# Loading float32 instead of casting in the DMA, in blocks of 8 heads with paired transposes: a change to a batched q·kᵀ kernel

## The chip, the cores and the metric

The kernel runs on one core of a Trainium2 chip. The metric is the device time in microseconds (us) of one execution. Times are medians of 4 executions for a changed kernel, and of 4 to 7 for the kernel before, which was run again on the same chip beside each group of experiments. In what follows PE is the engine that multiplies matrices, DVE (vector), ACT (scalar) and GpSimd (POOL in the profiles) are the engines that copy and convert here, and SP only issues transfers. SBUF is the memory on the chip, PSUM the one that PE writes to, and DMA stands for the transfers and the engines that carry them. A ratio is the mean time of one kernel's runs over that of the other's of the same rounds, so it is not quite the ratio of the medians that are quoted.

## The reference

```python
batch, n_heads, seq, head_dim = 8, 12, 1024, 64     # q and k: float32, 0.1 * normal
def reference(q, k):
    return np.einsum('bhid,bhjd->bhij', q, k).astype(np.float32)
```

There are 96 heads. Each takes 0.52 MB of input (q and k) and writes a 1024 x 1024 float32 matrix, 4.19 MB. In all 50.3 MB are read and 402.7 MB written.

## The kernel before

Inputs are loaded in batches of four heads (1, 1 and 2 at the start) by GpSimd, in a DMA that casts to float16 on the way. They are prefetched three batches ahead. PE transposes q and k through a 128 x 128 identity, DVE copies the transposed tiles from PSUM to SBUF, and PE multiplies. The contraction has only 64 rows, half of the array, so the kernel keeps a copy of k's transpose in both halves and lets even and odd output tiles use different halves. DVE empties three of eight output tiles, ACT five. Each head's 4 MB are stored by one DMA from SP.

```python
in_pool  = tc.tile_pool(name="in_pool", bufs=4)      # float16 inputs
out_pool = tc.tile_pool(name="out_pool", bufs=4)     # 4 heads of output, 4 MB each
...
def load(self):                                       # on GpSimd's queue, float32 -> float16
    nc.gpsimd.dma_start(out=dst[:, : self.R], in_=src[rows].rearrange("(p r) d -> p r d", p=P))
...
def transpose(self, a):                               # once per head: 4 + 16 matmuls
    for e in range(4):
        nc.tensor.transpose(t_ps[:, e], self.q_sb[:, r : r + 2], ident)
    for t in range(NT):
        nc.tensor.transpose(t_ps[0:64, 4 + t], rows, ident)
        nc.tensor.transpose(t_ps[64:128, 4 + t], rows, ident)
    ...                                               # DVE copies to qT and kT
def scores(self, g):
    for t in range(NT):
        h = (t % 2) * 64                              # halves of the array alternate
        for n in range(2):
            nc.tensor.matmul(ps[:, n * 512 : (n + 1) * 512], qT[h : h + 64, g, t // 2],
                             kT[h : h + 64, g, n * 512 : (n + 1) * 512])
        ...                                           # t in (1, 4, 6): DVE, else ACT
    nc.sync.dma_start(out=of[bh]..., in_=o_sb...)
```

## Time and profile before

| | before |
|---|---|
| time, median of 4 | 1071.33 us (1071.20 to 1072.24) |
| DMA queues, share of 16 engines | stores 88.0%, loads 11.9% |
| PE, DVE, ACT busy | 59%, 53%, 44% |
| PE on score matmuls | 480.9 us |
| four heads, while inputs are loaded | about 44 us |
| four heads, after the last load | about 39 us |

The first lines are from the page of the kernel before: busy time of the engines; the busy tenths of the DMA engines and their GB/s in 40 slices of the span; the queues (packets, MB, share); the chain of waits by engine; and three groups of instructions (busy time, mean ns of one, then idle time before them and its main releaser).

```profile
PE 627.9 (59%) x3456; PEld 214.0 (20%) x3456; DVE 565.7 (53%) x758; ACT 468.4 (44%) x481; POOL 28.2 (3%) x58
...
DMA  9999999999999999999999999999999999999996
GB/s 213 394 382 386 380 400 414 394 420 396 410 410 384 422 398 410 411 389 419 401 397 424 390 419 401 400 419 389 415 406 399 422 430 430 429 434 432 431 431 292
...
q1 hardware_dynamic: 13824, 402.66, 88.0%
q0 software_dynamic: 7488, 25.17, 11.9%
...
DMA 77%; PE 7%; ACT 7%; DVE 1%; issue 0%; ACTq 0%
...
L114 ACT COPY o_sb<-ps 128x1024 f32<-128x1024 f32 x480 | 467.1, 1014 | 566.5 <-DMA out_dram<-o_sb 359.1
L106 PE MATMUL ps<-kT,qT 64*128 64x512 f16 x1536 | 480.9, 597 | 270.8 <-ACT o_sb L114 227.2
L91 DVE COPY qT<-t_ps 128x128 f16<-128x128 f16 (+1 forms) x374 | 121.2, 469 | 95.7 <-PE t_ps L82 95.7
```

The DMA engines are the limit: nine tenths or more in every slice but the last, and 99.9% in the two queues together. ACT's idle time ends mostly when an output buffer has been stored ("DMA out_dram<-o_sb"), and PE waits for ACT. The compute engines have slack.

The next lines are from the chain of waits in order of time (start, length, what). Four heads lie between neighbours of each pair.

```profile
703.00 1.47 PE ps L106 x4
...
747.31 1.47 PE ps L106 x4
...
954.36 1.48 PE ps L106 x4
...
993.93 1.48 PE ps L106 x4
```

With loads, four heads take 44.3 us here (747.31 minus 703.00); after the last load they take 39.6 us. So eight heads with their loads cost the DMA about 88 us.

### The profile page before, as it was taken

What the parts mean: (1) busy time and instruction counts of PE and PEld (TensorE: products, weight loads), DVE (VectorE), ACT (ScalarE), POOL (GpSimd) and SP (SyncE); (2) the same over time, 40 slices, a digit from 0 to 9 for tenths busy, and PEclk for the clock granted to TensorE, in tenths of its full rate; (3) what the DMA queues carried; (4) which work ended last, traced back from release to release, by engine and by line L of the source; (5) the groups of instructions that cost most, each with busy time, mean ns of one, the idle gap of its engine ahead of it and who ended that gap; (6) DMA issues with size and microseconds to landing.
All of it is one profiled execution on the core that took longest, in us unless ns stands there. A gap on an engine that the chain in (4) does not pass through costs nothing.

```text
span 1069.6 us, 8844 instructions
## 1 busy us (share of the span) xinstructions
PE 627.9 (59%) x3456; PEld 214.0 (20%) x3456; DVE 565.7 (53%) x758; ACT 468.4 (44%) x481; POOL 28.2 (3%) x58
## 2 busy tenths in 40 slices
PE   6786455565654656557465564655656567667530
PEld 2222121121211212212122121221211212212100
DVE  5676445464653646547455464554655646655420
ACT  4454344444533445344443444444444445454530
POOL 3000000000000000000000000000000000000000
PEclk8565555555555555555555555555555555555555
DMA  9999999999999999999999999999999999999996
GB/s 213 394 382 386 380 400 414 394 420 396 410 410 384 422 398 410 411 389 419 401 397 424 390 419 401 400 419 389 415 406 399 422 430 430 429 434 432 431 431 292
DMA packets 21353, 428.39 MB, mean 401 GB/s; under 512 B 2368, under 2 KB 2880, under 8 KB 9024
## 3 DMA queue, kind: packets, MB, share of 16 engines
q1 hardware_dynamic: 13824, 402.66, 88.0%
q0 software_dynamic: 7488, 25.17, 11.9%
q8 instruction: 27, 0.44, 0.1%
q14 instruction: 14, 0.11, 0.0%
HBM read 50.33 MB, written 402.65 MB: 424 GB/s over the span
## 4 chain that ended last, share of the span: by engine, by line
DMA 77%; PE 7%; ACT 7%; DVE 1%; issue 0%; ACTq 0%
DMA out_dram<-o_sb 77%; ACT o_sb L114 7%; PE ps L106 6%; DVE kT L92 0%; DVE qT L91 0%; PE t_ps L81 0%; PE t_ps L78 0%; DVE o_sb L112 0%; PE t_ps L82 0%; ACTq L114 0%
## 5 line engine op out<-in xcount | busy, mean ns | idle before, releaser
L114 ACT COPY o_sb<-ps 128x1024 f32<-128x1024 f32 x480 | 467.1, 1014 | 566.5 <-DMA out_dram<-o_sb 359.1
L106 PE MATMUL ps<-kT,qT 64*128 64x512 f16 x1536 | 480.9, 597 | 270.8 <-ACT o_sb L114 227.2
L112 DVE COPY o_sb<-ps 128x1024 f32<-128x1024 f32 x288 | 351.7, 1223 | 374.0 <-DMA out_dram<-o_sb 213.8
L106 PEld LDWEIGHTS <-qT 64*128 64x128 f16 x1536 | 101.0, 109 | 605.2 <-issue 580.0
L91 DVE COPY qT<-t_ps 128x128 f16<-128x128 f16 (+1 forms) x374 | 121.2, 469 | 95.7 <-PE t_ps L82 95.7
L78 PE MATMUL t_ps<-ident,q_sb 128*128 128x128 f16 x384 | 56.4, 299 | 135.9 <-DVE kT L92 130.2
L92 DVE COPY kT<-t_ps 128x1024 f16<-128x1024 f16 x96 | 118.8, 1237 | 0.0
L81 PE MATMUL t_ps<-ident,k_sb 128*64 128x128 f16 x768 | 102.5, 310 | 0.0
L82 PE MATMUL t_ps<-ident,k_sb 128*64 128x128 f16 x768 | 102.4, 310 | 0.0
L81 PEld LDWEIGHTS <-k_sb 128*64 128x64 f16 x768 | 77.5, 165 | 19.8 <-issue 19.4
L82 PEld LDWEIGHTS <-k_sb 128*64 128x64 f16 x768 | 77.4, 164 | 7.5 <-issue 7.5
L78 PEld LDWEIGHTS <-q_sb 128*128 128x128 f16 x384 | 34.6, 127 | 187.2 <-issue 121.3
L64 POOL DMA_DIRECT2D q_sb<-in_q_dram x26 | 14.0, 537 | 767.5 <-PE t_ps L78 766.8
L64 POOL DMA_DIRECT2D k_sb<-in_k_dram x26 | 13.9, 534 | 13.2 <-PE t_ps L82 13.2
L114 ACT ACT_TABLE_LOAD x1 | 1.3, 1283 | 0.7 <-PEq L157 0.7
masks.py:199 POOL TENSOR_SCALAR_AFFINE_SELECT ident<-ident 128x128 f16<-128x128 f16 x1 | 0.4, 362 | 0.0
masks.py:197 POOL MEMSET ident<- 128x128 f16 x1 | 0.3, 271 | 0.0
L157 POOL MEMSET const-float32-0.0<- 128x1 f32 x1 | 0.1, 98 | 0.2 <-issue 0.2
L157 POOL MEMSET const-bfloat16-1.0<- 128x1 bf16 x1 | 0.1, 101 | 0.0
L157 POOL MEMSET const-uint8-127<- 128x1 uint8 x1 | 0.1, 101 | 0.0
L157 POOL MEMSET const-float32-1.0<- 128x1 f32 x1 | 0.1, 98 | 0.0
## 6 DMA issues: line engine op xcount, KB each, us to landing
out_dram<-o_sb SPq DMA_DIRECT2D x96, 4096.0 KB, 36.7
q_sb<-in_q_dram POOLq DMA_DIRECT2D x23, 512.0 KB, 18.1
k_sb<-in_k_dram POOLq DMA_DIRECT2D x23, 512.0 KB, 29.4
q_sb<-in_q_dram POOLq DMA_DIRECT2D x2, 128.0 KB, 3.5
k_sb<-in_k_dram POOLq DMA_DIRECT2D x2, 128.0 KB, 3.6
q_sb<-in_q_dram POOLq DMA_DIRECT2D x1, 256.0 KB, 6.3
k_sb<-in_k_dram POOLq DMA_DIRECT2D x1, 256.0 KB, 7.0
```

The costliest lines, as they stand in the source:

```text
L64: nc.gpsimd.dma_start(out=dst[:, : self.R], in_=src[rows].rearrange("(p r) d -> p r d", p=P),)
L78: nc.tensor.transpose(t_ps[:, e], self.q_sb[:, r : r + 2], ident)
L81: nc.tensor.transpose(t_ps[0:64, 4 + t], rows, ident)
L82: nc.tensor.transpose(t_ps[64:128, 4 + t], rows, ident)
L91: nc.vector.tensor_copy(out=qT[:, g, :, :, a], in_=t_ps[:, 0:4, ms])
L92: nc.vector.tensor_copy(out=kT[:, :, :, a], in_=t_ps[:, 4:12].rearrange("c t (g m) -> c g m t", g=G),)
L106: nc.tensor.matmul(ps[:, n * 512 : (n + 1) * 512], qT[h : h + 64, g, t // 2], kT[h : h + 64, g, n * 512 : (n + 1) * 512],)
L112: nc.vector.tensor_copy(out=o_sb[:, t], in_=ps)
L114: nc.scalar.copy(out=o_sb[:, t], in_=ps)
L157: nc = _bacc.Bacc("TRN2", target_bir_lowering=False, num_devices=1)
```

## The change

The intent, as far as the text of the change shows it, is to relieve PE, DVE and the casting DMA. Heads are taken in blocks of eight (2, 2 and 4 at the start), made of two halves of four. A transpose takes a row of a head from the first half beside the same row of a head from the second, 128 values wide, so two heads need 16 transposes instead of 40. Inputs are loaded as float32 by ACT's queue, one block-sized buffer (bufs=1), and GpSimd casts them to float16 just before they are transposed. Stores go out by SP and ACT in turn. The first three blocks are loaded into an output buffer that is not needed yet. A head's scores now use one half of the array for all its tiles.

```diff
-    in_pool = ctx.enter_context(tc.tile_pool(name="in_pool", bufs=4))
+    in_pool = ctx.enter_context(tc.tile_pool(name="in_pool", bufs=1))
+    half_pool = ctx.enter_context(tc.tile_pool(name="half_pool", bufs=2))
...
         def transpose(self, a):
+            t_ps = pt_pool.tile([P, 2 * NT, P], F16, tag="pt")
+            slab = slice(a * NT, (a + 1) * NT)
+            for i, src in enumerate((self.q_sb, self.k_sb)):
+                x_h = half_pool.tile([P, NT, 2, D], F16, tag=f"h{i}")
+                nc.gpsimd.tensor_copy(
+                    out=x_h, in_=src[:, :, slab].rearrange("p h t d -> p t h d")
+                )
+                for t in range(NT):
+                    nc.tensor.transpose(t_ps[:, i * NT + t], x_h[:, t], ident)
...
+            cs = slice(half * D, (half + 1) * D)
...
+                    nc.tensor.matmul(ps[:, js], qT[cs, g, t], kT[cs, g, js])
...
+            store = nc.sync if (self.first + n) % 2 == 0 else nc.scalar
...
+        for n in range(2 * b.G):
+            b.scores(n)
+            if nxt and done < nxt.G:
+                last = nxt.G if n == 2 else done + 1
+                while done < min(nxt.G, last):
+                    nxt.transpose(done)
+                    done += 1
+            if n == 3 and i + 2 < len(blocks):
+                blocks[i + 2].load(nc.scalar, nc.scalar)
```

The order of instructions on an engine is not the order of this text: the framework's scheduler decides it when the program is built.

More of the change, by code (lines that the diff above doesn't have):

```diff
@@ L28 @@
     GMAX = 4
-    assert D == 64 and NT == 8 and BH % GMAX == 0
+    assert D == 64 and NT == 8 and BH % (2 * GMAX) == 0
     qf = q.rearrange("b h s d -> (b h s) d")
@@ L37 @@
     of = out.rearrange("b h i j -> (b h) i j")
-    sizes = [1, 1, 2] + [GMAX] * (BH // GMAX - 1)
-    assert sum(sizes) == BH
+    sizes = [1, 1, 2] + [GMAX] * (BH // (2 * GMAX) - 1)
+    assert 2 * sum(sizes) == BH
     consts = ctx.enter_context(tc.tile_pool(name="consts", bufs=1))
     ident = consts.tile([P, P], F16)
-    in_pool = ctx.enter_context(tc.tile_pool(name="in_pool", bufs=4))
+    in_pool = ctx.enter_context(tc.tile_pool(name="in_pool", bufs=1))
+    half_pool = ctx.enter_context(tc.tile_pool(name="half_pool", bufs=2))
     tr_pool = ctx.enter_context(tc.tile_pool(name="tr_pool", bufs=2))
@@ L53, with place, load @@
     )
-    class Batch:
+    class Block:
         def __init__(self, first, G):
             self.first, self.G, self.R = first, G, 8 * G
-        def load(self):
-            rows = slice(self.first * S, (self.first + self.G) * S)
-            self.q_sb = in_pool.tile([P, GMAX * NT, D], F16, tag="q")
-            self.k_sb = in_pool.tile([P, GMAX * NT, D], F16, tag="k")
-            for src, dst in ((qf, self.q_sb), (kf, self.k_sb)):
-                nc.gpsimd.dma_start(
-                    out=dst[:, : self.R],
-                    in_=src[rows].rearrange("(p r) d -> p r d", p=P),
-                )
+        def place(self, q_sb, k_sb):
+            shape = dict(h=2, r=self.R, d=D)
+            self.q_sb = q_sb.rearrange("p (h r d) -> p h r d", **shape)
+            self.k_sb = k_sb.rearrange("p (h r d) -> p h r d", **shape)
+        def load(self, q_engine, k_engine):
+            if not hasattr(self, "q_sb"):
+                elems = 2 * self.R * D
+                q_sb = in_pool.tile([P, elems], F32, tag="q")
+                k_sb = in_pool.tile([P, elems], F32, tag="k")
+                self.place(q_sb, k_sb)
+            for half in range(2):
+                start = (self.first + half * self.G) * S
+                rows = slice(start, start + self.G * S)
+                for src, dst, eng in (
+                    (qf, self.q_sb, q_engine),
+                    (kf, self.k_sb, k_engine),
+                ):
+                    eng.dma_start(
+                        out=dst[:, half],
+                        in_=src[rows].rearrange("(p r) d -> p r d", p=P),
+                    )
         def alloc(self):
-            self.qT = tr_pool.tile([P, GMAX * 4 * P], F16, tag="qT")
+            self.qT = tr_pool.tile([P, GMAX * S], F16, tag="qT")
             self.kT = tr_pool.tile([P, GMAX * S], F16, tag="kT")
@@ L74, in transpose, with scores @@
             G, pp = self.G, P // self.G
-            t_ps = pt_pool.tile([P, 12, P], F16, tag="pt")
-            for e in range(4):
-                r = a * NT + 2 * e
-                nc.tensor.transpose(t_ps[:, e], self.q_sb[:, r : r + 2], ident)
-            for t in range(NT):
-                rows = self.k_sb[:, a * NT + t]
-                nc.tensor.transpose(t_ps[0:64, 4 + t], rows, ident)
-                nc.tensor.transpose(t_ps[64:128, 4 + t], rows, ident)
-            qT = self.qT[:, : G * 4 * P].rearrange(
-                "c (g e m a) -> c g e m a", g=G, e=4, m=pp
+            t_ps = pt_pool.tile([P, 2 * NT, P], F16, tag="pt")
[4 more added lines that the diff above has]
+                    out=x_h, in_=src[:, :, slab].rearrange("p h t d -> p t h d")
+                )
+                for t in range(NT):
+                    nc.tensor.transpose(t_ps[:, i * NT + t], x_h[:, t], ident)
+            qT = self.qT[:, : G * S].rearrange(
+                "c (g t m a) -> c g t m a", g=G, t=NT, a=G
             )
             kT = self.kT[:, : G * S].rearrange(
-                "c (g m a t) -> c g m a t", g=G, m=pp, t=NT
+                "c (g m a t) -> c g m a t", g=G, a=G, t=NT
             )
-            for g in range(G):
-                ms = slice(g * pp, (g + 1) * pp)
-                nc.vector.tensor_copy(out=qT[:, g, :, :, a], in_=t_ps[:, 0:4, ms])
+            nc.vector.tensor_copy(
+                out=qT[:, :, :, :, a],
+                in_=t_ps[:, :NT].rearrange("c t (g m) -> c g t m", g=G),
+            )
             nc.vector.tensor_copy(
                 out=kT[:, :, :, a],
-                in_=t_ps[:, 4:12].rearrange("c t (g m) -> c g m t", g=G),
+                in_=t_ps[:, NT:].rearrange("c t (g m) -> c g m t", g=G),
             )
-        def scores(self, g):
-            bh = self.first + g
-            qT = self.qT.rearrange("c (g e m) -> c g e m", e=4, m=P)
+        def scores(self, n):
+            half, g = divmod(n, self.G)
+            cs = slice(half * D, (half + 1) * D)
+            qT = self.qT.rearrange("c (g t m) -> c g t m", t=NT, m=P)
             kT = self.kT.rearrange("c (g j) -> c g j", j=S)
@@ L102, in scores @@
             for t in range(NT):
-                h = (t % 2) * 64
                 ps = po_pool.tile([P, S], F32, tag="po")
-                for n in range(2):
-                    nc.tensor.matmul(
-                        ps[:, n * 512 : (n + 1) * 512],
-                        qT[h : h + 64, g, t // 2],
-                        kT[h : h + 64, g, n * 512 : (n + 1) * 512],
-                    )
+                for j in range(2):
+                    js = slice(j * 512, (j + 1) * 512)
+                    nc.tensor.matmul(ps[:, js], qT[cs, g, t], kT[cs, g, js])
                 if t in (1, 4, 6):
@@ L114, in scores @@
                     nc.scalar.copy(out=o_sb[:, t], in_=ps)
-            nc.sync.dma_start(
-                out=of[bh].rearrange("(p t) j -> p (t j)", p=P),
+            store = nc.sync if (self.first + n) % 2 == 0 else nc.scalar
+            store.dma_start(
+                out=of[self.first + n].rearrange("(p t) j -> p (t j)", p=P),
                 in_=o_sb.rearrange("p t j -> p (t j)"),
             )
-    batches, first = [], 0
+    blocks, first = [], 0
     for G in sizes:
-        batches.append(Batch(first, G))
-        first += G
-    AHEAD = 3
-    for b in batches[:AHEAD]:
-        b.load()
-    make_identity(nc, ident)
-    batches[0].alloc()
-    for a in range(batches[0].G):
-        batches[0].transpose(a)
-    for i, b in enumerate(batches):
-        if i + AHEAD < len(batches):
-            batches[i + AHEAD].load()
-        nxt = batches[i + 1] if i + 1 < len(batches) else None
+        blocks.append(Block(first, G))
+        first += 2 * G
+    early_sb = out_pool.tile([P, NT, S], F32, tag="out")
+    early = early_sb.rearrange("p t j -> p (t j)")
+    at = 0
+    for b in blocks[:3]:
+        elems = 2 * b.R * D
+        b.place(early[:, at : at + elems], early[:, at + elems : at + 2 * elems])
+        at += 2 * elems
+    for b in blocks[:4]:
+        b.load(nc.sync, nc.scalar)
+    make_identity(nc, ident)
+    blocks[0].alloc()
+    blocks[0].transpose(0)
+    for i, b in enumerate(blocks):
+        nxt = blocks[i + 1] if i + 1 < len(blocks) else None
         if nxt:
             nxt.alloc()
-        for g in range(b.G):
-            b.scores(g)
-            if nxt:
-                for a in range(g * nxt.G // b.G, (g + 1) * nxt.G // b.G):
-                    nxt.transpose(a)
+        done = 0
+        for n in range(2 * b.G):
[7 more added lines that the diff above has]
+                blocks[i + 2].load(nc.scalar, nc.scalar)
 _INS = ['q', 'k']
```

## The prediction

> **What bounds the kernel now.** The DMA engines. The page's DMA slices read 9 in every tenth but the last, and the queue table gives 88.0% of the 16 engines' span to stores (402.66 MB) and 11.9% to loads. The chain of waits is 77% "DMA out_dram<-o_sb". PE is 59% busy, DVE 53%, ACT 44%; ACT's largest wait (359.1 us) is for an output buffer to be stored. From the chain, four heads take about 44.0 us while inputs are loaded and 39.3 us after the last load, so stores move at about 430 GB/s, and loading four heads (2.10 MB of float32 in HBM) costs about 4.7 us: the DMA already pays by bytes read, not by the float16 bytes written (estimate).
>
> **What the change does.**
> - *DMA.* Stores are untouched. Loads become 8 KB float32 rows without a cast; 2.10 MB at 430 GB/s is 4.9 us against 4.7 now (estimate). No gain, perhaps +0 to +4 us in all. Putting stores on two issuing queues gains nothing by itself: the Trainium skill ("DMA: Bandwidth & Descriptors", section "Issuing engines are not separate DMA queues") says that all queues run on the same 16 engines; this trace agrees, its two queues adding up to 99.9%.
> - *Transposes.* 1920 matmuls (20 per head) become 768 (16 per two heads); the DVE copies that empty them fall from 240 us to about 120 us.  Off the critical path.
> - *Scores.* Rows 0-63 and 64-127 of the array no longer alternate, so two matmuls no longer overlap. Now six 512-column matmuls take 1.92 us; alone each should take about 0.43 us at half clock (four times a 128-column transpose step of 0.105 us), so PE needs about 6.8 us per head and a head about 8 us instead of 6.7.
> - *GpSimd.* 96 casts of 128x1024, no duration in this trace; I assume 1 to 2 us each, 100 to 200 us, hidden.
> - *Bursts.* In the instruction order, three of a block's four transpose groups fall inside one head in eight. One group costs about 4.5 us (PE 2, DVE 2.5, one PSUM buffer), so that head takes some 20 us. Four output buffers hold 25 to 39 us of stores, nearly enough.
>
> **How much is on the critical path.** Almost nothing in the middle. At the start: a cast stands before the first transpose, and PE, DVE and the eleven groups of the first nine heads must keep up with 9.8 us per store; block 4's loads are issued only one to three heads before use. I expect the first store at about 22 us instead of 17.0, and 5 to 15 us of idle DMA in the first 150 us, partly paid back because float32 loads of 16 heads fill the first 20 us.
>
> **Predicted time.** 1074 us, range 1055 to 1100. Faster by over 2%: 0.03; within 2%: 0.81; slower by over 2%: 0.16.
>
> **What would show the steps right or wrong.** DMA slices still 9 throughout; about 44 us per four heads in the middle and 39.3 at the end; the DMA queue table near 88% and 11 to 12%; POOL 100 to 200 us; DMA dips, if any, before 150 us or at heads 8, 16, 24 and on.
>
> **What would make it wrong.** If GpSimd casts take 4 us or more, the bursts outlast the stores in flight and every block leaves a hole: 2 to 5% slower. If PE warms to full clock, bursts shrink and the time goes to 1065. If loads without a cast cost clearly less DMA time than 4.7 us per four heads, or the second queue lifts the rate above 430 GB/s, it could be over 2% faster; unlikely, since 453 MB at 430 GB/s are already 1053 us.

## The result, and the profile after

The changed kernel takes 1152.43 us (median of 4, 1151.28 to 1154.11): 7.6% slower (ratio 1.0756, interval 1.0738 to 1.0775). The prediction had said 1074 us, and 1055 to 1100.

The page of the changed kernel, the same lines as before, with the line of the DVE copy that moves q's transposes:

```profile
PE 757.0 (66%) x2304; PEld 286.3 (25%) x2304; DVE 510.6 (44%) x384; ACT 470.5 (41%) x481; POOL 98.1 (9%) x102
...
DMA  9969497989989989999998998998999899899998
GB/s 394 424 274 432 179 407 316 434 351 428 424 352 431 407 366 411 419 410 374 409 420 348 428 427 371 405 412 365 406 425 436 351 427 426 377 435 422 436 431 375
...
q10 hardware_dynamic: 13824, 247.47, 51.0%
q1 hardware_dynamic: 8064, 205.52, 42.6%
...
DMA 8%; PE 3%; DVE 1%; ACT 0%; issue 0%; ACTq 0%
...
L126 PE MATMUL ps<-kT,qT 64*128 64x512 f16 x1536 | 667.2, 624 | 126.3 <-DVE o_sb L128 104.9
L130 ACT COPY o_sb<-ps 128x1024 f32<-128x1024 f32 x480 | 469.3, 1014 | 642.9 <-PE ps L126 621.1
...
L107 DVE COPY qT<-t_ps 128x1024 f16<-128x1024 f16 x48 | 110.7, 2306 | 85.7 <-PE t_ps L99 85.7
```

The DMA now has holes, two or three slices apart. Its two queues fill 93.6% of 1150.3 us, that is 1077 us; before it was 99.9% of 1069.6, or 1069 us. So the time that packets took grew by 8 us, and some 73 us are new idle time. About 31 of them lie between 60 and 200 us (busy share 0.78), about 40 between 200 and 1000 us (busy share 0.95). ACT used to wait for the DMA to free output buffers; now 621.1 of its 642.9 idle us end with a matmul. (Shares of the chain don't add up to the span here, because the chain could not be followed back to the start; its 8% is not evidence.)

Who keeps PE waiting is shown by the waits of the changed kernel from 200 to 1000 us (who waited for whom: us in total, times, longest):

```profile
PE t_ps L99 <- POOL x_h L95: 120.3, 16, 14.2
PE ps L126 <- DVE o_sb L128: 79.5, 59, 2.0
PE t_ps L99 <- DVE kT L111: 56.4, 18, 3.7
```

The next line is of the view by stretches of time, for the same stretch and kernel: its ends and length, the busy us (and instructions) of PE, PEld, DVE, ACT and POOL, the granted clock, the DMA's busy share and its GB/s.

```profile
200.00:1000.00 800.00, 541.67 (x1657) 207.28 (x1656) 373.74 (x278) 334.43 (x343) 66.96 (x66) 1.00 0.95 401
```

PE's busy time and these three waits add up to 797.9 of 800 us. None of PE's waits ends with a store. In this stretch the kernel is a serial chain through PE, which is too slow for the DMA by some 5%. The timeline shows one turn of this chain (start, length, engine, line, operation, and in brackets the idle time before it and what ended it):

```profile
502.95 1.04 POOL L95 CAST x_h<-q_sb 128x1024 f16<-128x1024 f32 x1 [30.35 <-PE t_ps L99]
503.94 1.04 POOL L95 CAST x_h<-k_sb 128x1024 f16<-128x1024 f32 x1
...
507.31 1.89 PE L99 MATMUL t_ps<-ident,x_h 128*128 128x128 f16 x16 [2.62 <-DVE kT L111]
...
512.86 1.87 PE L99 MATMUL t_ps<-ident,x_h 128*128 128x128 f16 x16 [3.65 <-DVE kT L111]
...
523.93 0.35 ACTq L80 DMA_DIRECT2D q_sb<-in_q_dram  x1
...
533.70 0.35 ACTq L80 DMA_DIRECT2D k_sb<-in_k_dram  x1
...
542.05 0.35 ACTq L80 DMA_DIRECT2D q_sb<-in_q_dram  x1
543.76 0.33 ACTq L80 DMA_DIRECT2D k_sb<-in_k_dram  x1
...
561.55 2.03 POOL L95 CAST x_h<-q_sb 128x1024 f16<-128x1024 f32 x2 [56.57 <-DMA q_sb<-in_q_dram]
562.65 1.03 PE L99 MATMUL t_ps<-ident,x_h 128*128 128x128 f16 x8 [14.24 <-POOL x_h L95]
```

At 504.98 GpSimd has cast the last of a block, and its one input buffer is free. ACT issues the four loads for the next block only 19 to 39 us later, because they stand between its copies, and the last two just before 544. The data have landed at 561.5. PE wants to transpose them at 548.4 already and stands still for 14.24 us. Before that come the bursts: two groups of transposes back to back, each waiting for DVE's copies of the one before (2.62 and 3.65 us). A hole in the DMA follows. Two stretches of the same turn, in the view by stretches, with the columns given above:

```profile
516.00:520.00 4.00, 1.98 (x6) 0.60 (x5) 3.36 (x3) 1.93 (x2) 0.00 (x0) 1.00 0.02 8
...
568.00:572.00 4.00, 4.00 (x11) 1.37 (x10) 2.39 (x2) 2.52 (x3) 0.11 (x1) 1.00 0.48 205
```

The order of the built program explains why PE wants the data so early (PE's records in the trace come in the same order). A dot is one output tile of a head, T16 a group of 16 transposes, and the number tells the block that it is for (block 3 has heads 8 to 15, block 4 heads 16 to 23, block 5 heads 24 to 31, block 6 heads 32 to 39):

```
changed kernel, as built             as the program text states it
h16: .....T16(5) .T16(5) T16(5) ..   h16: ........T16(5)
h20: ....T16(6) ....                 h17: ........T16(5)
h24: .....T16(6) .T16(6) T16(6) ..   h18: ........T16(5) T16(5)
h28: ....T16(7) ....                 h24: ........T16(6)
```

The scheduler moved each block's first group four heads forward, to just behind its own loads (issued by ACT between its copies of heads 17 to 19 for block 6; the last of them 0.4 of a head before the transposes), and pushed the other three into one head.

### The profile page after: what moved, and what is told of

It reads as the page before. It is cut to its first block, busy times and chain, and to the rows that moved or that the text cites. A ratio compares the mean times of both kernels' runs of the same rounds, so it can differ in the third digit from the quotient of the medians.

```text
span 1150.3 us, 6260 instructions
## 1 busy us (share of the span) xinstructions
PE 757.0 (66%) x2304; PEld 286.3 (25%) x2304; DVE 510.6 (44%) x384; ACT 470.5 (41%) x481; POOL 98.1 (9%) x102
## 5 line engine op out<-in xcount | busy, mean ns | idle before, releaser
L126 PE MATMUL ps<-kT,qT 64*128 64x512 f16 x1536 | 667.2, 624 | 126.3 <-DVE o_sb L128 104.9
L130 ACT COPY o_sb<-ps 128x1024 f32<-128x1024 f32 x480 | 469.3, 1014 | 642.9 <-PE ps L126 621.1
L126 PEld LDWEIGHTS <-qT 64*128 64x128 f16 x1536 | 208.7, 138 | 555.1 <-issue 549.3
L99 PE MATMUL t_ps<-ident,x_h 128*128 128x128 f16 x768 | 93.1, 311 | 237.8 <-POOL x_h L95 161.4
L107 DVE COPY qT<-t_ps 128x1024 f16<-128x1024 f16 x48 | 110.7, 2306 | 85.7 <-PE t_ps L99 85.7
L99 PEld LDWEIGHTS <-x_h 128*128 128x128 f16 x768 | 77.5, 143 | 278.8 <-POOL x_h L95 173.1
L95 POOL CAST x_h<-q_sb 128x1024 f16<-128x1024 f32 x44 | 45.3, 1043 | 861.0 <-DMA q_sb<-in_q_dram 558.2
L111 DVE COPY kT<-t_ps 128x1024 f16<-128x1024 f16 x48 | 59.0, 1228 | 0.0
L95 POOL CAST x_h<-k_sb 128x1024 f16<-128x1024 f32 x44 | 45.3, 1043 | 8.2 <-PE t_ps L99 5.2
L95 POOL CAST x_h<-early_sb 128x1024 f16<-128x1024 f32 x8 | 8.1, 1043 | 8.0 <-DMA early_sb<-in_q_dram 4.8
```

Source lines behind the costliest of these rows:

```text
L95: nc.gpsimd.tensor_copy(out=x_h, in_=src[:, :, slab].rearrange("p h t d -> p t h d"))
L99: nc.tensor.transpose(t_ps[:, i * NT + t], x_h[:, t], ident)
L107: nc.vector.tensor_copy(out=qT[:, :, :, :, a], in_=t_ps[:, :NT].rearrange("c t (g m) -> c g t m", g=G),)
L111: nc.vector.tensor_copy(out=kT[:, :, :, a], in_=t_ps[:, NT:].rearrange("c t (g m) -> c g m t", g=G),)
L126: nc.tensor.matmul(ps[:, js], qT[cs, g, t], kT[cs, g, js])
L130: nc.scalar.copy(out=o_sb[:, t], in_=ps)
```

## The experiments

Theory A, after the result: a block of eight heads is a serial chain on PE of about 95 us, made of scores, transposes, a wait for loads and waits for DVE, against 88 us of DMA. Only the excess over 88 costs time, so taking away any large term should help. Rivals: B, the late loads alone make the loss; C, the score matmuls, which no longer overlap, make it alone; D, the bursts alone. All edits below are against the changed kernel unless said otherwise.

| run | edit | median us | ratio to before (95%) | PE's wait for casts, whole run |
|---|---|---|---|---|
| changed kernel | | 1152.43 | 1.0756 (1.0738 to 1.0775) | 161.4 us |
| e1 | halves of the array alternate (wrong result) | 1122.30 | 1.0477 (1.0459 to 1.0495) | 202.1 |
| e2 | PE in program order | 1074.54 | 1.0041 (1.0013 to 1.0069) | 10.6 |
| e3 | PE in order, four groups at once | 1078.92 | 1.0072 (1.0056 to 1.0087) | 6.4 |
| e4 | before, one half only (wrong result) | 1070.97 | 0.9998 (0.9981 to 1.0015) | |
| e5 | e2, first group right behind its loads | 1127.18 | 1.0522 (1.0506 to 1.0539) | 204.7 |
| e9 | e2, first group one head later than e5 | 1106.14 | 1.0329 (1.0313 to 1.0345) | 177.6 |
| e6 | e2, first group two heads later than e5 | 1071.87 | 1.0011 (0.9983 to 1.0039) | 137.8 |
| e7 | e2, loads issued by SP | 1072.39 | 1.0011 (0.9996 to 1.0026) | 6.7 |
| e8 | e2, all stores by SP | 1082.19 | 1.0103 (1.0086 to 1.0120) | 30.2 |
| e10 | loads issued by SP, order free | 1074.41 | 1.0033 (1.0016 to 1.0050) | 72.7 |

### e1: the halves of the array alternate again

```diff
+                    cs = slice((t % 2) * D, (t % 2 + 1) * D)
                     nc.tensor.matmul(ps[:, js], qT[cs, g, t], kT[cs, g, js])
```

The result is wrong (two heads are mixed); data flow and order stay.

> Wrong result on purpose. The changed kernel with one edit: the score matmuls of tile t use rows 0-63 for even t and 64-127 for odd t, so two can overlap again; instruction order and data flow stay. Theory A (sum): a block of 8 heads is a serial chain of about 95 us on PE (8 heads at about 8.2, 14 waiting for the next block's loads, 16 for three transposes groups in a row) against 88 us of DMA; any term taken away helps. It expects a head at about 6.7 us, so the time about 1085 to 1120. Rival B (late loads alone): 1140 or more, the PE only waits longer for the loads. Rival C (half-array matmuls alone): 1070 to 1085.

It took 1122.3 us, just above the band of theory A and well below that of rival B. PE's time on scores fell from 667.2 to 520.7 us, but its wait for casts rose from 161.4 to 202.1: a faster head comes sooner to the same late loads. Rival B had said 1140 or more, rival C 1070 to 1085; both miss. So the lost overlap is worth 30 us here, and is neither the whole cause nor without part.

### e2 and e3: PE in program order, spread or in one burst

Every PE instruction is pinned behind the one that the program states before it. In e3 the four groups of a block also come together, after the first head of the block before.

```diff
-                    nc.tensor.transpose(t_ps[:, i * NT + t], x_h[:, t], ident)
+                    ins = nc.tensor.transpose(t_ps[:, i * NT + t], x_h[:, t], ident)
+                    if True:
+                        tc.keep_in_program_order(ins)
...
-                    nc.tensor.matmul(ps[:, js], qT[cs, g, t], kT[cs, g, js])
+                    tc.keep_in_program_order(
+                        nc.tensor.matmul(ps[:, js], qT[cs, g, t], kT[cs, g, js])
+                    )
...
-                last = nxt.G if n == 2 else done + 1      # e3 only
+                last = nxt.G
```

> The changed kernel with the PE's instructions pinned to the order in which the program states them: the first transposes of a block then come after the first head of the block before it (4 heads later than in the changed kernel), and the four groups lie after heads 0, 1 and 2 instead of three in one head. Theory A: PE's wait for casts falls from 335 us to under 40, no holes in the DMA after 150 us, 1070 to 1090. Rival B expects the same. Rival C (half-array matmuls alone): 1130 or more.

> As the in-order kernel, but all four groups of a block come right after its predecessor's first head: a burst of about 22 us once in 8 heads, no wait for loads. Theory A: the chain is 8 times 8.2 plus 22, 88 us a block, about equal to the DMA: 1080 to 1110, with holes at the bursts. Rival B (late loads alone): as the spread kernel within 1%. Rival D (the bursts alone make the loss): 1150 or more.

PE's order alone takes the time from 1152.4 to 1074.5 us, with the same loads, casts and half-array matmuls. The loads are still issued late (for block 6 while PE is in heads 18 to 20), so an early issue is not what helps here. The 335 us of the expectation are the waits of PE and of its weight loads (PEld) for the same casts, added (161.4 and 173.1 us); PE's own are the ones in the table. Here is the page of e2:

```profile
DMA  9999999999999999999999999999999999999998
...
q10 hardware_dynamic: 13824, 247.47, 54.7%
q1 hardware_dynamic: 8064, 205.52, 44.6%
```

And its waits from 200 to 1000 us:

```profile
PE ps L129 <- ACT o_sb L134: 135.6, 40, 24.1
PE ps L129 <- DVE o_sb L132: 52.3, 45, 2.0
PE t_ps L99 <- DVE kT L113: 32.9, 9, 3.7
...
ACT o_sb L134 <- DMA out_dram<-o_sb: 143.5, 15, 24.6
```

The wait for casts is gone from this stretch. Instead PE waits for ACT, and ACT waits again for stores: the limit is the DMA, at 99.3% of the span. Rival C falls. The burst without the wait (e3) costs only some 4 us more, with one visible hole, so rival D falls too. But e3 lies 1 us under the band of theory A (1080 to 1110) and is what rival B expected, within 1% of e2. These two runs don't part A from B; e1 did, and e9 does below.

### e4: the kernel before with one half of the array

```diff
-                h = (t % 2) * 64
+                h = 0
```

> Wrong result on purpose. The kernel before with one edit: all score matmuls use rows 0-63, so none overlap, as in the changed kernel; everything else stays. Theory A: a head with its transposes grows from 8.6 to about 10.3 us, still under the DMA's 11.0: 1071 to 1085. Rival C (half-array matmuls alone): 1130 or more.

It took 1070.97 us, the same as before (ratio 0.9998), though PE worked much longer on its scores. The group of score matmuls on its page:

```profile
L106 PE MATMUL ps<-kT,qT 64*128 64x512 f16 x1536 | 672.1, 628 | 98.7 <-ACT o_sb L114 90.0
```

The 191 us added (480.9 to 672.1) went into slack. The same loss of overlap costs nothing in a kernel whose chain is below the DMA's budget, and 30 us in one whose chain is above it (e1). This is what theory A says and rival C does not.

### e5, e9 and e6: how many heads lie between loads and first transposes

Starting from e2, the PE part of a block's first group comes after head `m` of the block two before it; its copies by DVE stay where they were (for this the method `transpose` is split in two, which is not shown). With m = 3 (e5) it follows right on the last load, with 4 (e9) one head later, with 5 (e6) two heads; in e2 there are five.

```diff
+            if n == 3 and i + 2 < len(blocks):            # 3, 4 or 5
+                blocks[i + 2].transpose_pe(0)
```

> The in-order spread kernel (1074.5 us) with one thing moved: the first transposes of a block (PE part only, their copies stay) come after the fourth head of the block two before it, that is right after its last load is issued, so with 0 heads of lead instead of 5. If the wait for the loads makes the loss, PE waits for casts about 20 us a block, the chain is about 78 plus 20 us against 88 of DMA, and the time is 1130 to 1180. If the order of PE's work matters for another reason than the lead of the loads, nothing tells this kernel from the next: both equal.

> The same with 2 heads of lead (after the sixth head). If the lead is what counts: PE waits 0 to 6 us a block, the chain stays under 88 us and the time is 1073 to 1085. Rival: as the kernel with 0 heads of lead.

> The in-order spread kernel with a block's first transposes after the fifth head of the block two before it: 1 head of lead, where the changed kernel has them too (in the middle of that head), but without its burst of three groups in one head. With 0 heads it was 1127, with 2 heads 1072. If wait and burst share one budget (a chain of at most 88 us a block costs nothing), the wait of about 12 us alone gives a chain of about 88 to 92 and 1075 to 1105, clearly under the changed kernel's 1152, though the burst alone cost only 4 us (1079 against 1074.5). If the wait alone makes the loss and the burst adds its 4 us, it is 1140 or more.

The times are 1127.2, 1106.1 and 1071.9 us for 0, 1 and 2 heads: 21 and 34 us per head of lead, then nothing more (e2: 1074.5). The expected bands were missed by little: e5 by 3 us, e6 and e9 by 1 us. In e6 and e9 the edit doesn't reach block 4, which keeps the place that it has in e2.

Here rival B falls. e5 and e9 have no burst, and their lead of 0 and 1 heads lies on both sides of the changed kernel's 0.4. The late loads alone cost 56 and 35 us over the kernel before, not 81; B had said 1140 us or more for e9. The changed kernel, which has the burst too, is 25 us slower than e5 and 46 slower than e9, though the burst costs only 4 us where there is no wait (e3).

The waits of e6 from 200 to 1000 us tell more than the time:

```profile
PE t_ps L104 <- POOL x_h L100: 125.1, 16, 15.5
PE ps L136 <- DVE o_sb L139: 51.4, 53, 2.0
PE t_ps L104 <- DVE kT L120: 32.9, 9, 3.7
```

The view by stretches of e6, for the same stretch:

```profile
200.00:1000.00 800.00, 579.68 (x1729) 218.33 (x1728) 389.19 (x292) 365.41 (x370) 64.74 (x65) 1.00 1.00 428
```

PE waits for casts about as long as in the changed kernel (125.1 against 120.3 us), and yet the DMA is full. The waits for DVE differ: 51.4 and 32.9 us here, 79.5 and 56.4 with the burst. So a wait for loads is no loss in itself: it costs only what it puts the chain over the budget, together with the burst's waits. The expectation that e6's waits would shrink to 6 us a block was wrong: when the DMA is full, loads take longer to land (median 31 us in e6 for both inputs, 15 and 20 us in the changed kernel), and the slack turns into waiting.

The chain of PE per eight heads can be worked out from the same two views of a stretch in which both kernels still load inputs, 200 to 850 us. The scale is the number of score matmuls of that stretch, 128 for eight heads: 875 in the changed kernel and 944 in e6, that is 6.84 and 7.38 times eight heads. All times in the table are those of the 650 us divided by these numbers.

| per eight heads, us | changed | e6 |
|---|---|---|
| PE busy | 63.3 | 63.4 |
| wait for casts, that is loads | 15.5 | 14.8 |
| wait for DVE to empty score tiles | 9.7 | 5.6 |
| wait for DVE to copy transposes | 6.4 | 4.0 |
| wait for ACT to empty score tiles | none listed | 0.3 |
| sum | 94.9 | 88.1 |
| length (650 us divided by the number) | 95.1 | 88.1 |

So e6 runs at the DMA's 88 us, and the changed kernel at 7 us above it. Of these, 6.5 are waits for DVE and 0.7 the wait for loads. That does not clear the loads: in e6 their wait takes up what slack there is, and is not itself the limit. A turn of the changed kernel read directly from one store's issue (519.42) to that of the same head of the next block (614.93) took 95.5 us: PE was busy for 63.1 of them, and waited 16.5 for casts, 9.4 for DVE to empty score tiles and 6.3 for DVE to copy transposes.

### e7 and e8: who issues loads and stores, PE in order

```diff
-                blocks[i + 2].load(nc.scalar, nc.scalar)       # e7
+                blocks[i + 2].load(nc.sync, nc.sync)
...
-            store = nc.sync if (self.first + n) % 2 == 0 else nc.scalar   # e8
+            store = nc.sync
```

> The in-order spread kernel with the later loads issued by SP, which has nothing else to do than stores, instead of between ACT's copies. Loads go out as soon as the casts free the buffer; the wait of 12 us for block 4's loads at 88 us should shrink, ACT gets 15 us back. 1066 to 1074, PE's waits for casts under 20 us in all. If SP's in-order queue lets loads hold up stores (a load that waits for casts blocks an even store), 1080 or more.

> The in-order spread kernel with all stores on SP again, loads alone on ACT. The skill's statement that all queues share the same 16 engines says no change in rate: within 0.5% of 1074.5, DMA busy share 99%. If two queues of stores move more bytes per us than one, it is slower by over 1%.

The skill's statement meant there is that of the section named at the end of this part.

e7 is as fast as the kernel before (1072.4 us, inside its band). e8 fits neither expectation: 1082.2 us, 0.7% slower than e2. The view by stretches shows where. First e8 from 200 to 1000 us and from 100 to 150 us:

```profile
200.00:1000.00 800.00, 577.13 (x1735) 217.07 (x1735) 388.03 (x290) 363.18 (x366) 66.81 (x66) 1.00 1.00 430
...
100.00:150.00 50.00, 22.78 (x99) 11.04 (x100) 18.41 (x13) 9.93 (x10) 8.04 (x8) 1.00 0.76 311
```

And e2 from 200 to 1000 us:

```profile
200.00:1000.00 800.00, 578.57 (x1725) 216.08 (x1723) 388.97 (x290) 363.17 (x368) 66.37 (x66) 1.00 1.00 424
```

In the long middle the rate is no lower with one store queue than with two (430 and 424 GB/s), so a second queue moves no more bytes. The 12 us of idle DMA (24% of 50 us) lie in one hole near the start, where the first reload landed late: its last part was issued at 73.31 us, and the cast that waited for it began at 119.84. In e2 these loads were issued later (74.0 to 92.1 us) and no hole followed. Why they took so long in e8 no run shows. The Trainium skill ("DMA: Bandwidth & Descriptors", section "Issuing engines are not separate DMA queues") says that DMAs of all issuing engines run on the same 16 engines and interleave; these runs agree.

### e10: the loads issued by SP, nothing else

This is the changed kernel with e7's edit alone; the scheduler was free to order PE.

> The changed kernel with one edit: later loads issued by SP, order of PE left to the scheduler. In the built program the loads go out right after the last cast, but the first transposes of the next block move forward with them, to 1 to 2 heads after their loads. If the lead over the transposes is what counts, and not when a load is issued, PE still waits 10 us or more a block and the time is 1100 to 1150. If late issue between ACT's copies was the cause, it is under 1085.

Of the two outcomes the second came: 1074.4 us, under 1085. One edited line takes back 78 of the 81 us. The timeline of e10:

```profile
539.77 1.04 POOL L95 CAST x_h<-k_sb 128x1024 f16<-128x1024 f32 x1
539.85 0.34 SPq L80 DMA_DIRECT2D q_sb<-in_q_dram  x1
...
542.69 1.20 SPq L80 DMA_DIRECT2D k_sb<-in_k_dram  x1
...
566.34 2.03 POOL L95 CAST x_h<-q_sb 128x1024 f16<-128x1024 f32 x2 [25.53 <-DMA q_sb<-in_q_dram]
567.44 0.71 PE L99 MATMUL t_ps<-ident,x_h 128*128 128x128 f16 x5 [7.77 <-POOL x_h L95]
```

SP issues only these loads and half of the stores, and all four loads are out within 4 us of the cast that frees the buffer, where ACT needed 39. From the last cast to the first of the next block it is 25.5 us instead of 56.6. PE still waits, but 7.8 us instead of 14.2, with the burst still there; the chain is then under the budget (the two queues fill 99.4% of the span).

The edit also changed PE's order: the scheduler put the first transposes three heads earlier still (in head 17 for block 6, by the order of PE's records). So this run does not show early loads with everything else held. What differs is the lead. From the last load's issue to the moment when PE wants the data it is 17.0 us here (542.69 to 559.67), with two groups of the burst inside it, and 4.7 us in the changed kernel (543.76 to 548.41). So a short lead between loads and transposes makes the loss, and the burst makes it larger. Moving the transposes (e2, e6) or issuing the loads sooner (e10) gives the lead back.

## Why the prediction was wrong

- **Right: the DMA bounds the kernel before, and its work hardly changes.** Estimated: 0 to 4 us more for the loads. Measured: 1077 us of DMA time instead of 1069 in the changed kernel, 1064 in e2 (99.3% of 1071.8). The rate in the middle stayed at about 430 GB/s of stores and loads together when the DMA was full.
- **Right: a score head on PE, with overlap gone.** Predicted about 6.8 us of PE and 8 us a head. Sixteen matmuls in one piece took 6.74 to 6.98 us, and two heads took 15.1 us between two stores of ACT (578.37 and 593.49). That this alone costs nothing was right (e4).
- **Right: GpSimd's casts are hidden.** 1.04 us each, 98 us in all for POOL, against 1 to 2 us assumed. The prediction had named a hole in every block as a risk, but for slow casts, which is not what happened. The Trainium skill ("GPSIMD Engine Reference", section 4.1) calls one-input work on GpSimd roughly line rate; 1024 elements per partition in 1.04 us are, as an estimate, about 1.2 cycles each at the 1.2 GHz that the page gives in section 1, which agrees with that.
- **Mis-sized: a group of transposes.** Estimated 4.5 us, "PE 2, DVE 2.5". The copy of q alone takes 2.31 us on average, where 2.5 were allowed for both copies, and a group in a burst takes 5.55 us (507.31 to 512.86). DVE's copies fell to 170 us (110.7 and 59.0), not 120. The trace of before held a warning: a copy of 128 columns with the same step of four elements took 0.47 us, more than one of 512 columns without a step (0.42 us).
- **Wrong, the step that failed: "Almost nothing in the middle."** The prediction saw that block 4's loads were issued one to three heads before use, and counted this once, for the start. The same order holds in every block: the first transposes of each block stand four heads early, behind loads that ACT cannot issue before its turn. No term of the sum had a wait for loads. It measured 120.3 us from 200 to 1000 us (15.5 for eight heads between 200 and 850 us), and with the burst it puts PE's chain at 95 us for eight heads, above the 88 us of the DMA. That left the DMA idle for about 40 us in the middle, where the prediction had almost none. Without the early group the kernel takes 1074.5 us (e2). That this is the predicted 1074 is luck in the digit: that sum also had idle time at the start, and e2's DMA is full there.
- **Wrong: the buffers as cover.** "Four output buffers hold 25 to 39 us of stores, nearly enough" is true of one burst, if the queue is full when it starts (e3). It is not true when the average of the chain exceeds the DMA's: then the queue doesn't refill, and ACT has no wait for a store between 200 and 1000 us.
- **Right in place, too small: the start.** First store at 20.7 us (predicted about 22). The DMA's busy share from 60 to 150 us was 0.73 in the changed kernel, 24 us idle, where 5 to 15 had been expected for the first 150 us. In that stretch PE waited 16.5 us for casts and 14.4 us for DVE to copy transposes, so loads and bursts share in it, as in the middle.

What stays open: why the scheduler moved the first group. The likely reason is that its model takes the loads as landed sooner than they are, but no run shows that. Open too is the size of each share: wait and burst were not taken away one by one with the loads held. And no version here beats the kernel before: e6, e7 and before agree within 0.2%, with the DMA full in all three.

## What to carry to other kernels

Give the chain of work per block a budget, which is the time of the engine that bounds it, and add up everything serial in it: busy time, waits for loads, bursts. Below the budget a term costs nothing (191 us of PE in e4), above it every microsecond counts, and slack hides each term until the last one is added. Read the order of the built program for every block, not for the one that looks odd, and ask of each instruction that reads loaded data how long before it the load is issued. Look which engine issues a load, and what stands before the load in that engine's order: here ACT's copies did, and SP had room.

## What the Trainium skill lacked or had wrong

- "DMA: Bandwidth & Descriptors", section "Issuing engines are not separate DMA queues": it says that issuing from several engines saves only sequencer time, usually small beside the DMA itself. That is so for the rate (424 and 430 GB/s). It has no figure for what the choice of engine did here: on ACT, between its copies, four loads went out 19 to 39 us after their buffer was free, on SP within 4 us, and that edit, with the new order of PE that came with it, was worth 78 us of 1152 (e10).
- "TensorE: Matmul & The Clock Gate", Part 1: it warns that clock events in a trace can be unreliable, and gives 426.7 ns for a 512-column matmul cold and 215.7 ns warm. These runs bear the warning out. Profiles of the changed kernel granted 1.0 in three runs and 0.519 in one, with the same time (1151.3 to 1154.1 us), and under a granted 1.00 sixteen such matmuls took 6.74 to 6.98 us, 0.42 to 0.44 us each. In these traces the time from one matmul to the next is what can be read, not the clock column.
- "SBUF — State Buffer", the note on 16-byte lines in "Door 1": it says that two hits per line are enough for full bandwidth. DVE's copies of 128x1024 float16 from PSUM took 1.29 us where the destination steps by two elements and 2.43 us where it steps by four, which still has two hits in 16 bytes. (The runs read from the source also halve, from 64 elements to 32, and no run parts the two.) No page was found that prices a step of four for 2-byte elements.
